# Another order for the seven products of a fast matrix product: the early pairs run M6, M7, M5, then M4 of the pair before, then M3

## The chip, the core and the metric

The kernel runs on one core of a Trainium2 chip. The metric is the device time of one launch in microseconds (us). The time before is 2344.93 us, the median of three runs (2343.69 to 2345.63).

## The reference

It is one layer of an encoder for two groups of tokens, 512 (`prompt`) and 1024 (`sample`), with shared weights and a width of 1024. A mixer with a convolution branch and a long-convolution branch comes first, then an MLP of width 4096. All is float32. The part that matters here is the first matrix of the MLP:

```
h = _ln(x) * (1.0 + scale2) + shift2
f = jnp.square(jax.nn.relu(jnp.einsum('bld,df->blf', h, mlp_w1[l]) + mlp_b1[l]))
f = jnp.einsum('blf,fd->bld', f, mlp_w2[l]) + mlp_b2[l]
x = _ln(DEEPNORM_ALPHA * x + gate2 * f, ln2_g[l], ln2_b[l])
```

## The kernel before

The kernel goes through both groups' mixers, then the MLP of the small group, and last the MLP of the large one. This last part is `up_seven` (the matrix `mlp_w1`, "up") and `down_seven` (`mlp_w2`). Both replace eight block products by seven, as Strassen's scheme does: tokens, contraction and output columns are each halved, and the seven products M1 to M7 work on sums and differences of the quarters (the table `SEVEN` names the weight piece and the token piece of each).

`up_seven` treats the 4096 output columns in 16 pairs n of two blocks of 128. One product is 12 matmuls of 128x512: four chunks of the contraction, and three matmuls for each, since a float32 operand is held as a high and a low part (`mm3`, and `split`, which makes the high part on ScalarE and the low part on VectorE). The token pieces are ready once (`h2_second`, tiles `pg`); the weight pieces of a pair are made by `up_weights` one to two pairs ahead, from four loads of 256 KB (tiles `raw` for even pairs, `xr` for odd ones): A11, A12, S1 and S2 in tiles `wt`, S3, S4 and A22 in tiles `pg`.

For the 14 early pairs (`NE`) the first loop does M1 and M2 already; M1 is written to the DRAM buffer `d_xs`, and the finished first block to `d_p`. The second loop fetches M1 back as `x` (line 1342, tile `sg`) and the block as `p11` (line 1357). It uses two accumulators in PSUM: `a` (tag `mm`) takes M6, then M5, then M3 on top of each other, and VectorE reads it after each of them (`keep()` gives `y` = x + M6 and `z` = x + M6 + M5, both tiles `xt`, and `p21` = x + all three, a tile `so`). `c` (tag `fx`) takes M7, is read for `p22`, then takes M4 on top and is read by `finish` for the block of slot 1. ScalarE applies the squared ReLU in two steps to every block, and the blocks and three sums of them (`s1`, `s2` and the `s4` of `finish`, tiles `sg`) are written to `d_p` by the queue of SyncE (`put`, line 1269). All DMAs of this part are issued by that one queue, in its order.

The order in the code is not the order on the engines. A scheduler puts every engine's instructions in a fixed row when the program is built, by priority (the place in the code; `soon` raises it) and by what its own model holds ready; buffers are given out at the same time. A product may so run earlier or later than it is written.

Of the kernel before, what the change touches and what calls it, by code (L numbers as in the profile page):

```python
# [173 lines left out]
class Enc:  # L174
# [1086 lines left out]
    def up_seven(self, g):  # L1261

        nc, v = self.nc, self.V
        put = lambda n, slot, t: nc.sync.dma_start(g.d_p[n, :, slot], t)
        NP = 16  # L1270
        ws = {n: {} for n in range(NP)}

        def c11(n, x, b):
            t = self.so()
            v.tensor_tensor(t, x, b, op=ALU.add)
            self.relu2(2 * n, t, t)
            put(n, 0, t)
            return t

        sums = self.h2_second(g, g.ss)  # L1280
        for n in range(NE):
            with self.soon(HW):
                for i in range(2):
                    ws[n]["A1" + "12"[i]] = self.piece(self.up_quarter(n, 0, i))
            for k in (1, 2):
                ps = self.mm_ps()
                self.up_product(g, ws[n], k, ps, True)
                if k == 1:
                    x = self.sg()
                    nc.scalar.activation(x, ps, AF.Copy)  # L1290
                    nc.sync.dma_start(g.d_xs[n], x)
                else:
                    c11(n, x, ps)
                if n >= NE - 6:
                    if n == NE - 6 and k == 1:
                        self.flush()
                    next(sums, None)
                yield 2.6
        self.flush()
        preps = {n: self.up_weights(n, ws[n], n >= NE) for n in range(NP)}  # L1300
        next(preps[0])
        next(preps[1])
        for _ in range(7):
            next(preps[0])
            next(sums, None)
        for _ in sums:
            pass
        last = None
        for n in range(NP):
            w = ws[n]  # L1310
            step = lambda: next(preps[n + 1], None) if n + 1 < NP else None
            early = n < NE
            a = self.mm_ps()

            def keep():
                t = self.xt()
                if early:
                    v.tensor_tensor(t, x, a, op=ALU.add)
                else:
                    nc.scalar.activation(t, a, AF.Copy)  # L1320
                return t

            def finish(last):
                y, c, s2, w0 = last
                self.up_product(g, w0, 4, c, False)
                t = self.so()
                v.tensor_tensor(t, y, c, op=ALU.add)
                f = 2 * n - 1
                self.relu2(f, t, t)
                put(n - 1, 1, t)  # L1330
                if s2 is not None:
                    s4 = self.sg()
                    v.tensor_tensor(s4, t, s2, op=ALU.subtract)
                    put(n - 1, 6, s4)

            if n + 2 < NP:
                with self.soon(20):
                    next(preps[n + 2])
            if early:
                x = self.sg()  # L1340
                with self.soon(40):
                    nc.sync.dma_start(x, g.d_xs[n])
            else:
                self.up_product(g, w, 1, a, True)
                x = keep()
            step()
            if last:
                finish(last)
                yield 2.6
            step()  # L1350
            self.up_product(g, w, 6, a, early)
            y = keep()
            step()
            if early:
                p11 = self.so()
                with self.soon(40):
                    nc.sync.dma_start(p11, g.d_p[n, :, 0])
                yield 0.0
            else:
                b = self.mm_ps()  # L1360
                self.up_product(g, w, 2, b, True)
                p11 = c11(n, x, b)
                yield 2.6
            step()
            self.up_product(g, w, 5, a, False)
            z = keep()
            yield 2.6
            step()
            c = self.fx_ps()
            self.up_product(g, w, 7, c, True)  # L1370
            p22 = self.so()
            v.tensor_tensor(p22, z, c, op=ALU.add)
            self.relu2(2 * n + 1, p22, p22)
            put(n, 5, p22)
            yield 2.6
            step()
            self.up_product(g, w, 3, a, False)
            p21 = self.so()
            if early:
                v.tensor_tensor(p21, x, a, op=ALU.add)  # L1380
                self.relu2(2 * n, p21, p21)
            else:
                self.relu2(2 * n, a, p21)
            s2 = None
            if n < N7:
                s1, s2 = self.sg(), self.sg()
                v.tensor_tensor(s1, p21, p22, op=ALU.add)
                put(n, 4, s1)
                v.tensor_tensor(p21, p11, p21, op=ALU.subtract)
                v.tensor_tensor(s2, s1, p11, op=ALU.subtract)  # L1390
                put(n, 2, s2)
            put(n, 3, p21)
            yield 2.6
            step()
            last = (y, c, s2, w)
        n = NP
        finish(last)
        yield 2.6
# [213 lines left out]
    def step(self, lane):  # L1612

        t = self.V.us
        try:
            next(self.side[lane][0])
        except StopIteration:
            self.side[lane].pop(0)
        self.spent[lane] += (self.V.us - t) / LANES[lane]
# [208 lines left out]
```

## Time and profile before

| what | value |
|---|---|
| median of three runs | 2344.93 us |
| the profiled execution | 2339.18 us, its span 2337.2 us |
| TensorE busy | 2238.0 us, 96% of the span |
| VectorE busy | 1904.4 us, 81% |
| ScalarE busy | 921.6 us, 39% |
| the second loop of `up_seven`, from pair 0 to pair 13 | 1773.39 to 1975.55 us of the span |

PE is TensorE, DVE is VectorE, ACT is ScalarE, SP is SyncE, whose queue issues the DMAs. In the rows further down the time of an instruction's start comes first, then its duration, and in brackets how long its engine had nothing to do before it and what ended that. Matmuls of one tile are merged into one row (x12). All of DVE's and PE's instructions have line 157, so they are told apart by their tiles: `xt<-sg,mm` is y or z, `so<-sg,mm` is p21, `so<-xt,fx` is p22 or the block of `finish`, `sg<-so` is s1.

### The profile page before, as it was taken

To read this page: it belongs to the slowest core of one execution; us is meant where nothing else is said; L and a number is where in the kernel's file an instruction comes from. 1 tells how busy PE (TensorE), PEld (TensorE's weight loads), DVE (VectorE), ACT (ScalarE), POOL (GpSimd) and SP (SyncE) were. 2 spreads that over 40 slices of the span, in tenths; PEclk is the share of its full clock that TensorE was granted. 3 is DMA by queue.
4 is the path that set the end of the run, shared out by engine and by line. 5 is a ranking of instruction groups with operands and counts; after the bars stand their busy time and mean duration, and the time that the engine had idled before them with its cause. 6 is when DMAs were issued, how large, how long until landed. Compare 5 with 4: busy or idle time off the path is not lost.

```text
span 2337.2 us, 32839 instructions
## 1 busy us (share of the span) xinstructions
PE 2238.0 (96%) x11492; PEld 1850.7 (79%) x11492; DVE 1904.4 (81%) x3694; ACT 921.6 (39%) x1521; POOL 54.0 (2%) x149
## 2 busy tenths in 40 slices
PE   6999999999999989979999999999999999999998
PEld 3878777787878877868888888789887777788886
DVE  5989798877989988888988877965988777577888
ACT  3464522422222223456443335222575345444430
POOL 2210100000000000000000000000000000000000
PEclk9999999999999999989999999999999999999999
DMA  6556425574446666534443326643675666876631
GB/s 246 180 159 189 138 79 188 196 240 155 153 149 211 217 213 219 191 129 139 138 128 107 121 77 234 207 149 117 223 238 185 207 214 212 287 247 206 216 117 69
DMA packets 201066, 414.34 MB, mean 177 GB/s; under 512 B 23321, under 2 KB 33739, under 8 KB 200389
## 3 DMA queue, kind: packets, MB, share of 16 engines
q1 hardware_dynamic: 200069, 411.24, 53.3%
q8 instruction: 90, 1.47, 0.3%
q0 software_dynamic: 832, 1.02, 0.2%
q14 instruction: 75, 0.61, 0.1%
HBM read 317.73 MB, written 94.43 MB: 176 GB/s over the span
## 4 chain that ended last, share of the span: by engine, by line
PE 74%; DVE 13%; DMA 7%; ACT 3%; issue 2%; SPq 1%; DVEq 0%; ACTq 0%
PE mm L157 55%; PE fx L157 16%; DVE fp L157 3%; PE tr L157 3%; DVE sg L157 2%; DVE pg L157 2%; DVE wt L157 2%; DMA sg<-d_xs 1%; DMA fp<-in_w_ada_dram 1%; DMA sg<-ks 1%; DVE st L157 1%; DVE cv L157 1%; DVE xt L157 1%; DVE sm L157 1%; DMA sg<-d_t 1%
## 5 line engine op out<-in xcount | busy, mean ns | idle before, releaser
L157 PE MATMUL mm<-pg,wt 128*128 128x512 f32 (+1 forms) x4776 | 1144.9, 392 | 13.2 <-ACT pg L214 5.1
L157 PEld LDWEIGHTS mm<-pg,wt 128*128 128x128 f32 x4776 | 878.9, 189 | 208.0 <-issue 17.3
L157 PE MATMUL mm<-wt,pg 128*128 128x512 f32 (+1 forms) x2556 | 486.3, 346 | 12.3 <-DVE pg L157 7.8
L157 PEld LDWEIGHTS mm<-wt,pg 128*128 128x128 f32 x2556 | 405.6, 191 | 71.4 <-DVE pg L157 9.7
L214 ACT ACTIVATE wt<-raw 128x512 fp32r<-128x512 f32 x430 | 268.4, 630 | 450.7 <-PE mm L157 357.8
L157 DVE TENSOR_TENSOR wt<-raw,wt 128x512 fp32r<-128x512 f32 x430 | 289.0, 683 | 55.5 <-ACT wt L214 53.9
L157 DVE SCALAR_TENSOR_TENSOR cv<-cv,pp 128x1024 f32<-128x1024 f32 (+1 forms) x288 | 289.1, 1009 | 10.9 <-ACT cv L851 7.0
L157 PEld LDWEIGHTS fx<-fp,fft 128*128 128x128 f32 x1536 | 180.4, 193 | 17.2 <-issue 8.9
L157 PE MATMUL fx<-fp,fft 128*128 128x128 f32 x1536 | 186.0, 278 | 2.0 <-DMA fft<-in_fft_sig_dram 0.8
L157 DVE TENSOR_TENSOR fp<-fp 128x256 f32<-128x256 f32 (+2 forms) x352 | 154.9, 476 | 24.9 <-ACT fp L380 14.6
L157 DVE TENSOR_TENSOR sg<-fx,sg 128x512 f32<-128x512 f32 (+1 forms) x162 | 98.4, 629 | 41.7 <-PE fx L157 26.7
L157 DVE TENSOR_TENSOR pg<-so,pg 128x512 fp32r<-128x512 f32 (+1 forms) x162 | 99.5, 624 | 38.7 <-ACT pg L214 32.8
L157 PE MATMUL fx<-pg,pg 128*128 128x512 f32 x492 | 119.6, 391 | 6.8 <-ACT pg L214 4.3
L157 PEld LDWEIGHTS fx<-pg,pg 128*128 128x128 f32 x492 | 92.6, 189 | 26.7 <-ACT pg L214 4.7
L214 ACT ACTIVATE pg<-so 128x512 fp32r<-128x512 f32 (+1 forms) x127 | 72.3, 576 | 90.9 <-DVE so L157 57.3
L157 PE MATMUL fx<-wt,pg 128*128 128x512 f32 x387 | 95.6, 389 | 0.3 <-DVE so L157 0.3
L1258 ACT ACTIVATE so<-so,pp 128x512 f32<-128x512 f32 x62 | 44.4, 719 | 130.3 <-DVE so L157 130.2
L157 DVE TENSOR_TENSOR sg<-sg 128x256 f32<-128x256 f32 (+2 forms) x187 | 82.0, 460 | 7.8 <-ACT sg L888 6.7
L157 PEld LDWEIGHTS fx<-wt,pg 128*128 128x128 f32 x387 | 72.6, 188 | 15.7 <-DVE so L157 0.7
L157 PE MATMUL mm<-pg,pg 128*128 128x512 f32 x300 | 73.9, 395 | 5.5 <-DVE xt L157 5.5
L380 ACT ACTIVATE fp<-fx 128x512 f32<-128x512 f32 x48 | 28.7, 598 | 123.7 <-PE fx L157 123.6
L157 DVE TENSOR_TENSOR pg<-pg,pg 128x1024 fp32r<-128x1024 f32 (+1 forms) x45 | 55.0, 1222 | 22.0 <-ACT pg L214 17.7
(175 smaller groups left out, 2163.1 us busy)
## 6 DMA issues: line engine op xcount, KB each, us to landing
raw<-in_mlp_w_dram SPq DMA_DIRECT2D x232, 256.0 KB
raw<-in_w_in_dram SPq DMA_DIRECT2D x144, 256.0 KB
xr<-in_mlp_w_dram SPq DMA_DIRECT2D x104, 256.0 KB
fp<-in_w_ada_dram SPq DMA_DIRECT2D x48, 512.0 KB
pg<-d_p SPq DMA_DIRECT2D x44, 512.0 KB
raw<-in_w_out_dram SPq DMA_DIRECT2D x64, 256.0 KB
d_p<-so SPq DMA_DIRECT2D x64, 256.0 KB
d_g<-so SPq DMA_DIRECT2D x48, 256.0 KB
```

Of the source, the lines that this page charges most:

```text
L157: return f(*args, **kw)
L214: self.nc.scalar.activation(hi, src, AF.Copy)
L380: nc.scalar.activation(outs[-1][:, 4 * (pr % 2):4 * (pr % 2) + 4].rearrange("p (j w) c -> p j w c", j=2), ps, AF.Copy)
L1258: nc.scalar.activation(out, src, AF.Relu, bias=self.pp[:, C_B1 + f:C_B1 + f + 1], scale=1.0)
```

## The change

For early pairs the code now writes M7 directly behind M6 instead of behind M5, and it calls `finish` of the pair before (M4, its sum, its ReLU and its two writes) behind the second block of the pair, in front of M3, instead of at the head of the pair. What is done stays the same.

```
-            if last:
+            if last and not early:
                 finish(last)
                 yield 2.6
             step()
...
                 with self.soon(40):
                     nc.sync.dma_start(p11, g.d_p[n, :, 0])
-                yield 0.0
+                c = self.fx_ps()
+                self.up_product(g, w, 7, c, True)
             else:
                 b = self.mm_ps()
                 self.up_product(g, w, 2, b, True)
                 p11 = c11(n, x, b)
-                yield 2.6
+            yield 2.6
             step()
             self.up_product(g, w, 5, a, False)
             z = keep()
             yield 2.6
             step()
-            c = self.fx_ps()
-            self.up_product(g, w, 7, c, True)
+            if not early:
+                c = self.fx_ps()
+                self.up_product(g, w, 7, c, True)
             p22 = self.so()
             v.tensor_tensor(p22, z, c, op=ALU.add)
             self.relu2(2 * n + 1, p22, p22)
             put(n, 5, p22)
+            if last and early:
+                finish(last)
             yield 2.6
```

TensorE, from pair 4 or so to pair 13, before: the last four rows of each name a token tile. 16893 ends M6 and the four `fx` rows are M7, both of pair n + 1; the four rows with 16606 to 16922 are M5, then M3 and M4, of pair n.

```order
L157 MATMUL mm<-pg_16893,wt 128x512 x3
L157 MATMUL fx<-pg_16610,pg_17657 128x512 x3
L157 MATMUL fx<-pg_16718,pg_17657 128x512 x3
L157 MATMUL fx<-pg_16818,pg_17657 128x512 x3
L157 MATMUL fx<-pg_16926,pg_17657 128x512 x3
L157 MATMUL mm<-pg_16606,wt 128x512 x3
L157 MATMUL mm<-pg_16714,wt 128x512 x3
L157 MATMUL mm<-pg_16814,wt 128x512 x3
L157 MATMUL mm<-pg_16922,wt 128x512 x3
L157 MATMUL mm<-pg,pg_17555 128x512 x12
L157 MATMUL fx<-pg,pg_17582 128x512 x12
```

The same place after the change:

```order
L157 MATMUL mm<-pg_16893,wt 128x512 x3
L157 MATMUL fx<-pg_16610,pg_17650 128x512 x3
L157 MATMUL fx<-pg_16718,pg_17650 128x512 x3
L157 MATMUL fx<-pg_16818,pg_17650 128x512 x3
L157 MATMUL fx<-pg_16926,pg_17650 128x512 x3
L157 MATMUL mm<-pg_16606,wt 128x512 x3
L157 MATMUL mm<-pg_16714,wt 128x512 x3
L157 MATMUL mm<-pg_16814,wt 128x512 x3
L157 MATMUL mm<-pg_16922,wt 128x512 x3
L157 MATMUL mm<-pg,pg_17555 128x512 x12
L157 MATMUL fx<-pg,pg_17582 128x512 x12
```

Nothing moved here but the number of a tile. Rows of TensorE moved only in the first four pairs, where M7 and M4 change places with parts of M6 and M5.

VectorE in one pair, before, from y and z (the first row) to s1 (the last). `raw` and `wt` rows make the weight pieces, and the row with 17657 is the low part of S3.

```order
L157 TENSOR_TENSOR xt<-sg,mm 128x512 x2
L157 TENSOR_TENSOR xt<-raw 128x512
L157 TENSOR_TENSOR so<-xt,fx 128x512
L157 TENSOR_TENSOR raw<-raw 128x512
L157 TENSOR_TENSOR raw<-xt,raw 128x512
L157 TENSOR_TENSOR pg_17657<-raw,pg_17657 128x512
L157 TENSOR_TENSOR so<-sg,mm 128x512
L157 TENSOR_TENSOR wt<-raw,wt 128x512
L157 TENSOR_TENSOR raw<-raw 128x512
L157 TENSOR_TENSOR wt<-xt,wt 128x512
L157 TENSOR_TENSOR sg<-so 128x512
```

The same place after the change:

```order
L157 TENSOR_TENSOR xt<-sg,mm 128x512 x2
L157 TENSOR_TENSOR xt<-raw 128x512
L157 TENSOR_TENSOR so<-xt,fx 128x512 x2
L157 TENSOR_TENSOR raw<-raw 128x512
L157 TENSOR_TENSOR raw<-xt,raw 128x512
L157 TENSOR_TENSOR so<-sg,mm 128x512
L157 TENSOR_TENSOR sg<-so,sg 128x512
L157 TENSOR_TENSOR wt<-raw,wt 128x512
L157 TENSOR_TENSOR raw<-raw 128x512
L157 TENSOR_TENSOR wt<-xt,wt 128x512
L157 TENSOR_TENSOR sg<-so 128x512
L157 TENSOR_TENSOR pg_17650<-raw,pg_17650 128x512
```

The sum of `finish` (the second `so<-xt,fx`) and its s4 (`sg<-so,sg`) now stand ahead of s1, where both stood behind it, and the low part of S3 went from ahead of s1 to directly behind it. Behind z, s1 was the tenth instruction and is the eleventh.

The queue of SyncE in one pair, before: the block p22, two weight loads, p11, s1, and then the load of x for the next pair, with what follows it.

```order
L1269 DMA d_p_95<-so 128x512
L1216 DMA raw<-in_mlp_w_dram 128x512 x2
L1357 DMA so<-d_p_95 128x512
L1269 DMA d_p_95<-sg 128x512
L1342 DMA sg<-d_xs_96 128x512
L1269 DMA d_p_95<-sg 128x512
L1269 DMA d_p_95<-so 128x512 x2
L1269 DMA d_p_95<-sg 128x512
L1216 DMA raw<-in_mlp_w_dram 128x512 x2
```

The same place after the change, from the load of p11 on (it comes at the end of the pair before now):

```order
L1357 DMA so<-d_p_95 128x512
L1269 DMA d_p_95<-so 128x512 x2
L1269 DMA d_p_95<-sg 128x512
L1216 DMA raw<-in_mlp_w_dram 128x512
L1269 DMA d_p_95<-sg 128x512
L1216 DMA raw<-in_mlp_w_dram 128x512
L1342 DMA sg<-d_xs_96 128x512
L1269 DMA d_p_95<-sg 128x512
L1269 DMA d_p_95<-so 128x512
L1216 DMA raw<-in_mlp_w_dram 128x512 x2
```

The two writes of `finish` and p11 went ahead, and one weight load now stands between the write of s1 and the load of x. That weight load refills the tile that the low part of S3 is made from, and so waits for that VectorE instruction.

## Rows read from the trace of the kernel before

**Rows 1.** Busy time in the fourteen early pairs: stretch, length, engines, clock, DMA share
```profile
1773.39:1975.55 202.16, 191.57 (x819) 151.76 (x818) 147.23 (x237) 86.35 (x147) 0.00 (x0) 1.00 0.61 203
```
**Rows 2.** Timeline of TensorE, one pair: M3, M4, M6, M7, M5
```profile
1866.96 3.01 PE L157 MATMUL mm<-pg,pg 128*128 128x512 f32 x12 [0.78 <-DVE xt L157]
1869.81 2.88 PE L157 MATMUL fx<-pg,pg 128*128 128x512 f32 x12
1872.53 2.88 PE L157 MATMUL mm<-pg,wt 128*128 128x512 f32 x12
1875.25 2.88 PE L157 MATMUL fx<-pg,pg 128*128 128x512 f32 x12
1879.26 3.04 PE L157 MATMUL mm<-pg,wt 128*128 128x512 f32 x12 [1.13 <-DVE xt L157]
```
**Rows 3.** Timeline of VectorE, the same pair: z, p21, s1, the next y
```profile
1866.21 0.69 DVE L157 TENSOR_TENSOR xt<-sg,mm 128x512 f32<-128x512 f32 x1 [3.10 <-PE mm L157]
...
1870.07 0.68 DVE L157 TENSOR_TENSOR so<-sg,mm 128x512 f32<-128x512 f32 x1
...
1872.48 0.68 DVE L157 TENSOR_TENSOR sg<-so 128x512 f32<-128x512 f32 x1
...
1878.52 0.69 DVE L157 TENSOR_TENSOR xt<-sg,mm 128x512 f32<-128x512 f32 x1 [1.75 <-DMA sg<-d_xs]
```
**Rows 4.** Timeline of SyncE's queue, the same pair: s1, then x
```profile
1873.19 0.33 SPq L1269 DMA_DIRECT2D d_p<-sg  x1
1873.56 0.42 SPq L1342 DMA_DIRECT2D sg<-d_xs  x1
```
**Rows 5.** Waits of VectorE, y on x's load: total, times, longest
```profile
DVE xt L157 <- DMA sg<-d_xs: 12.9, 12, 2.1
```
**Rows 6.** Chain that ended last: three loads of x, start and length
```profile
1781.59 3.95 DMA sg<-d_xs
...
1873.56 4.93 DMA sg<-d_xs
...
1904.82 5.09 DMA sg<-d_xs
```
**Rows 7.** Timeline of VectorE: z of pair 0 and of pair 12
```profile
1773.39 0.69 DVE L157 TENSOR_TENSOR xt<-sg,mm 128x512 f32<-128x512 f32 x1 [2.03 <-PE mm L157]
...
1959.71 0.69 DVE L157 TENSOR_TENSOR xt<-sg,mm 128x512 f32<-128x512 f32 x1 [3.25 <-PE mm L157]
```
**Rows 8.** Timeline of ScalarE, the pair of rows 2: the squares of p21
```profile
1871.64 0.63 ACT L1259 ACTIVATE so<-so 128x512 f32<-128x512 f32 x1
```
**Rows 9.** Timeline of SyncE's queue, pair 11: s1, a weight load, x
```profile
1951.74 0.33 SPq L1269 DMA_DIRECT2D d_p<-sg  x1
1952.34 0.33 SPq L1216 DMA_DIRECT2D xr<-in_mlp_w_dram  x1
1952.73 0.45 SPq L1342 DMA_DIRECT2D sg<-d_xs  x1
```
**Rows 10.** Timeline of VectorE, pair 11: z and the next y
```profile
1943.90 0.69 DVE L157 TENSOR_TENSOR xt<-sg,mm 128x512 f32<-128x512 f32 x1 [3.15 <-PE mm L157]
...
1955.78 0.69 DVE L157 TENSOR_TENSOR xt<-sg,mm 128x512 f32<-128x512 f32 x1 [0.46 <-DMA sg<-d_xs]
```
**Rows 11.** Table of a stretch just behind an issue of x
```profile
1874.46:1875.21 0.75, 0.75 (x5) 0.63 (x4) 0.75 (x2) 0.69 (x2) 0.00 (x0) 1.00 0.97 363
```
**Rows 12.** Timeline of TensorE: starts behind its two longest gaps in this part
```profile
1762.44 1.22 PE L157 MATMUL fx<-pg,pg 128*128 128x512 f32 x2 [4.26 <-ACT pg L214]
...
2010.45 3.02 PE L157 MATMUL fx<-pg,pg 128*128 128x512 f32 x12 [2.50 <-DVE so L157]
```
**Rows 13.** Table of the stretches around the first gap and behind the early pairs
```profile
1758.00:1763.00 5.00, 0.74 (x2) 0.50 (x2) 5.00 (x10) 2.20 (x5) 0.00 (x0) 0.75 0.71 238
...
1975.55:2010.00 34.45, 32.41 (x142) 26.13 (x140) 19.34 (x28) 20.12 (x34) 0.00 (x0) 1.00 0.87 284
2010.00:2337.00 327.00, 316.41 (x1392) 261.08 (x1392) 253.13 (x400) 120.07 (x173) 0.00 (x0) 0.99 0.55 183
```

More of the change, by code (lines that the diff above doesn't have):

```diff
@@ L1346, in up_seven @@
             step()
-            if last:
+            if last and not early:
                 finish(last)
@@ L1357, in up_seven @@
                     nc.sync.dma_start(p11, g.d_p[n, :, 0])
-                yield 0.0
+                c = self.fx_ps()
+                self.up_product(g, w, 7, c, True)
             else:
@@ L1362, in up_seven @@
                 p11 = c11(n, x, b)
-                yield 2.6
+            yield 2.6
             step()
@@ L1368, in up_seven @@
             step()
-            c = self.fx_ps()
-            self.up_product(g, w, 7, c, True)
+            if not early:
+                c = self.fx_ps()
+                self.up_product(g, w, 7, c, True)
             p22 = self.so()
@@ L1374, in up_seven @@
             put(n, 5, p22)
+            if last and early:
+                finish(last)
             yield 2.6
```

## The prediction

> **What bounds the kernel now.** The table of stretches comes first. From z of pair 0 to z of pair 13 TensorE works 191.57 of 202.16 us at a granted clock of 1.00 [rows 1]. So 10.6 us of gaps is all that a new order can win there while the matmuls stay.
>
> The timeline of TensorE shows where they are [rows 2]. In the scheduled row M7 already stands between M6 and M5 before the change, and so does the row of the next pairs. Two gaps are left in a pair: 0.78 us ahead of M3, which waits for VectorE to read z out of the accumulator that M3 adds to, and 1.13 us ahead of M5, which waits for y. M3, M4, M6 and M7 follow without a gap, about 2.72 us apart.
>
> VectorE's timeline tells why y is late [rows 3]: it starts 1.75 us after VectorE was free, released by the load of x. The waits add up to 12.9 us in 12 of 13 cases [rows 5], so M5's gap is x's landing, not the product M6 that y also reads (over by 1875.4 [rows 2]). The queue of SyncE shows what x stands behind [rows 4]: s1's write at 1873.19, then x at 1873.56. That write waits for s1 on VectorE, which ends at 1872.48 + 0.68 = 1873.16 [rows 3].
>
> So one ring sets a pair's length: z, the VectorE row up to s1, s1's write, x's issue, x's landing, y, M5, the next z. The chain of waits runs through these loads [rows 6], the first at 1781.59. Pair 0 to pair 12 takes (1959.71 − 1773.39)/12 = 15.53 us a pair [rows 7]. From y to z it is 3.8 us (M5's 3.04, with 0.74 to its start and a little behind it [rows 2, 3]), which leaves 11.70 from z to y. The twelve loads, from the first [rows 6] to the last [rows 9], are issued 7.68 us after z on average. The earliest is 7.35 (1873.56 − 1866.21 [rows 3, 4]); the first is 8.20 (1781.59 − 1773.39 [rows 6, 7]); the last 8.83 [rows 9, 10]. The rest, 4.02 us on average, passes from issue to y; it is 5.1 at most (4.96 and 5.12 for the two long loads [rows 6]) and 3.05 at least (1955.78 − 1952.73 [rows 9, 10]).
>
> **The change part by part.**
>
> M7 ahead of M5: nothing. The row on TensorE in a steady pair is the same before and after. The 13 gaps of 0.78 us ahead of M3 (10 us) are therefore not won: M3 and M4 still come as M5, M3, M4 and the accumulator is still read between M5 and M3. In the first four pairs M7 and M4 change places with parts of M6 and M5; each product is as long as any other, so this adds or removes one such gap at most, ±0.8 us, taken as 0.
>
> VectorE: the sum of `finish` and s4 now stand ahead of s1, S3's low part went behind it, net one more instruction. Between p21 and s1 the row goes on in steps of (1872.48 − 1870.07)/4 = 0.60 us [rows 3]. s1 before starts 6.27 after z in the pair shown, so 6.87 now, and ends at 7.55.
>
> ScalarE: one more instruction of the ReLU goes ahead of p21's square, which ends at 1872.27 [rows 8], 6.06 after z. With one instruction of some 0.55 us more it ends at 6.6, before 6.87, so s1 does not wait for it. If that margin of 0.27 is gone it is 0.3 us a pair at most, inside the bounds below.
>
> SyncE: s1's write goes at 7.57. Behind it the changed queue has a weight load ahead of x, and this load refills the tile that the low part of S3 reads. That instruction now comes directly behind s1: start 7.47, end 8.15. So the weight load is issued at 8.17, and x 0.39 us behind it, as in pair 11, where a weight load already stood there (1952.73 − 1952.34 [rows 9]): 8.56. Against the mean of 7.68 x goes out 0.88 us later. The other writes that moved ahead of s1 (p22, `finish`, s4) wait for work that is done earlier and don't hold x up. Queued behind the waiting weight load are x and the writes for which nobody on TensorE waits. S3's low part itself is ready at 8.15 after z; M7 which reads it starts at 1875.25 − 1866.21 = 9.04 [rows 2, 3]: 0.9 us of margin.
>
> The landing decides the sign, and the trace shows no pair of exactly this kind. The nearest rows bound it. From below: pair 11, the one with a weight load between s1's write and x, has 3.05 us to y, and the sum is 8.56 + 3.05 = 11.61, 0.09 less than now, −1.1 us in 12 pairs. From above: if the landing keeps its mean of 4.02, each pair is 0.88 longer, +10.6 us; with the longest, 5.12, it is 1.98, +23.8 us. Which is nearer? Lateness alone does little: the eight loads issued at 7.35 to 7.51 take 4.22 on average, the three at 8.0 to 8.2 take 4.04 (the first [rows 6], with 0.09 to y), 4.23 and 3.13. Pair 11 is nearer for its neighbours: in the pair of rows 4 there is nothing between the write and x, in pair 11 there is the weight load, as in the change. One row is thin, so I weigh it two to one against the mean: (2 × 3.05 + 4.02)/3 = 3.37. Then y comes at 11.93, +0.23 a pair, 12 × 0.23 = +2.8 us.
>
> Behind x the DMA engines are nearly full: 0.97 busy at 363 GB/s just after an issue [rows 11]. So the landing is a time in a crowd and no fixed latency.
>
> The Trainium skill has a rule for this, in "DMA: Bandwidth & Descriptors", section "Queues, rings and completion order": the mark by which a DMA reports its end is strongly ordered, so on each DMA engine it lands only when every earlier write of that engine has landed. By it x, issued 0.37 us behind a write to DRAM [rows 4], inherits that write's end, and inherits less now that the write is 0.99 us ahead with a load between. By it the sum would be that of pair 11, −1.1 us; the trace agrees in that one pair [rows 9, 10], and the rule alone does not say how much of the 4.02 us it explains.
>
> The time lost or won here goes to the end in full. Behind the early pairs TensorE is busy 32.41 of 34.45 and 316.41 of 327.00 us [rows 13], so nothing there takes up a delay. The clock: behind a gap of 4.26 us the first two matmuls took 1.22 us, and the stretch was granted 0.75, the level below full speed [rows 12, 13]; behind 2.50 us twelve matmuls took 3.02, as in any pair, and the clock stayed at 0.99 [rows 12, 13]. M5's gap grows from 1.13 to some 1.4 us by this estimate and to 3.1 at the worst bound, so I cost the clock at 0.
>
> The sum against the profiled execution: 2339.18 + 2.8 = 2342.0. That execution is 5.75 us below the median of the runs; on the median it is 2344.93 + 2.8 = **2347.7 us**.
>
> **The rivals.**
>
> A, slower: the landing does not shorten. x goes out 0.88 us later in each of 12 pairs and y follows: +10.6 us, 2355.5. For it: the two loads issued at 8.2 were 0.85 us later than most and landed no faster, and the same bytes are moved in a pair, so the crowd may be as thick. Against it: pair 11, and that the write stands farther ahead of x. It decides as soon as the landing exceeds 3.53 (8.56 + 3.53 is 0.39 over now, 4.7 us).
>
> B, faster: the crowd around x gets thinner. The two writes of `finish` and that of p22 now go out before s1, and p11's load after, so fewer bytes are in flight when x is. If x then needs under 2.7 us, y comes at 11.25 or before, −0.45 a pair, −5.4 us: 2339.5. The floor is TensorE: M7 ends at 1875.25 + 2.72 = 1877.97, 11.76 after z, M5 starts 0.74 behind y, so y before 11.02 wins nothing: −0.68 × 12 = −8.2, 2336.8. For it: the best landing seen is 3.05 with the weight load between. Against it: no landing in twelve was below that.
>
> C, the change does what its words say: M5, M4, M3 in turn, the 0.78 us ahead of M3 goes, −10 us, 2335. Against it: the scheduled row. Or the load of p11 now waits at the end of a pair for a write to land and blocks the queue: up to +10 us. Either is a way in which a step of mine would be wrong altogether.
>
> **How the numbers follow.** A measurement of this kernel can't tell less than about 0.2% (4.7 us) from no change. The forecast case, landing between 2.8 and 3.55 us, 0.44, nearly all of it within 0.2%: 2342 to 2350. A 0.35, all slower. B 0.16, faster, C 0.05, half and half. That gives faster 0.16 + 0.02 with little of the forecast case, 0.19; slower 0.35 + 0.03 and the upper edge of the forecast case, 0.40; the same 0.41. The range goes from 2338, which leaves out half of B, to 2357, which takes in A at the mean landing and leaves out its long landings: some 0.18 outside.
>
> **What would show it right or wrong.** In the changed kernel's profile: M3 still waits 0.78 us; x is issued some 8.5 us after z, directly behind a weight load, which is behind s1's write; from issue to y 3.4 us; z to z 15.75 us; y's waits for x still in nearly all pairs. The forecast is wrong if x leaves before 8.0 or after 9.2 after z, if y stops waiting for x, if M6 or M7 waits for a weight piece (`pg` or `wt`), or if TensorE's clock falls below 0.99 in a stretch of these pairs.

## The result and the profile after

The changed kernel takes 2354.94 us (median of six runs, 2348.28 to 2363.89), the kernel before 2344.31 in the same comparison (six runs): 10.6 us more, a ratio of 1.0054 with a 95% interval of 1.0037 to 1.0070. It is slower, by half a percent. The forecast was 2347.7 us; the range, 2338 to 2357, holds the time, but what came is the size of rival A and not of the likeliest case.

The profiled execution of the changed kernel took 2355.90 us, 16.7 more than that of before. That is more than the medians differ by: the execution of before lies 5.1 us under its median, the one of the changed kernel 1.0 over. The longest landing and two of the three slow starts of TensorE shown below did not come in a second profiled execution of the same instructions (`finish` alone, next section).

The table of stretches from z of pair 0 to z of pair 13, columns as in [rows 1], and one short stretch for later:

```profile
1773.94:1989.13 215.19, 196.27 (x820) 154.38 (x819) 145.92 (x236) 80.90 (x145) 0.00 (x0) 0.98 0.58 190
1886.00:1892.00 6.00, 5.42 (x12) 3.77 (x12) 0.54 (x1) 0.00 (x0) 0.00 (x0) 0.54 0.26 85
```

The fourteen pairs are 13.0 us longer (215.19 against 202.16 [rows 1]) for the same work, and the granted clock is no longer 1.00 throughout.

TensorE in one ordinary pair of the changed kernel, M3, M4, M6, M7, M5 as in [rows 2]:

```profile
1855.61 3.02 PE L157 MATMUL mm<-pg,pg 128*128 128x512 f32 x12 [0.78 <-DVE xt L157]
1858.47 2.88 PE L157 MATMUL fx<-pg,pg 128*128 128x512 f32 x12
1861.19 2.88 PE L157 MATMUL mm<-pg,wt 128*128 128x512 f32 x12
1863.91 2.88 PE L157 MATMUL fx<-pg,pg 128*128 128x512 f32 x12
1867.20 3.01 PE L157 MATMUL mm<-pg,wt 128*128 128x512 f32 x12 [0.41 <-DVE xt L157]
```

The row is that of before, with the wait of 0.78 us ahead of M3 still in it: what the change says it does has not happened on this engine. From pair 5 to pair 12 TensorE's row is the same in both kernels.

VectorE in the same pair: z, p21, s1, the low part of S3, the next y. These answer to [rows 3]:

```profile
1854.87 0.69 DVE L157 TENSOR_TENSOR xt<-sg,mm 128x512 f32<-128x512 f32 x1 [3.10 <-PE mm L157]
...
1858.67 0.69 DVE L157 TENSOR_TENSOR so<-sg,mm 128x512 f32<-128x512 f32 x1
...
1861.68 0.69 DVE L157 TENSOR_TENSOR sg<-so 128x512 f32<-128x512 f32 x1
1862.28 0.69 DVE L157 TENSOR_TENSOR pg<-xr,pg 128x512 fp32r<-128x512 f32 x1
...
1866.46 0.69 DVE L157 TENSOR_TENSOR xt<-sg,mm 128x512 f32<-128x512 f32 x1 [1.07 <-DMA sg<-d_xs]
```

And the queue of SyncE, s1's write, the weight load, x, as in [rows 4]:

```profile
1862.40 0.32 SPq L1269 DMA_DIRECT2D d_p<-sg  x1
1863.00 0.33 SPq L1216 DMA_DIRECT2D xr<-in_mlp_w_dram  x1
1863.38 0.44 SPq L1342 DMA_DIRECT2D sg<-d_xs  x1
```

s1 starts 6.81 us after z (6.27 in [rows 3]). Its write goes 7.53 after z (6.98 before), and x goes 0.98 behind the write (0.37 before), because the weight load between waits for S3's low part, which ends at 1862.97. x leaves 8.51 us after z.

VectorE's waits for x in pairs 0 to 12, columns as in [rows 5], then three landings of x from the chain that ended last, as in [rows 6]:

```profile
DVE xt L157 <- DMA sg<-d_xs: 23.1, 12, 4.4
```

```profile
1863.38 3.05 DMA sg<-d_xs
...
1878.76 6.41 DMA sg<-d_xs
...
1915.76 4.52 DMA sg<-d_xs
```

y waits 23.1 us for x instead of 12.9. Most landings are short now (3.05 here), but some are long. Behind three long waits TensorE starts slowly; its timeline, M5 of two pairs and one product behind the early pairs:

```profile
1885.93 5.49 PE L157 MATMUL mm<-pg,wt 128*128 128x512 f32 x12 [3.77 <-DVE xt L157]
...
1921.04 4.51 PE L157 MATMUL mm<-pg,wt 128*128 128x512 f32 x12 [1.88 <-DVE xt L157]
...
2024.76 4.54 PE L157 MATMUL fx<-pg,pg 128*128 128x512 f32 x12 [3.44 <-DVE so L157]
```

Twelve matmuls take 5.49 and 4.51 us instead of 3.0, and the granted clock from 1886 to 1892 is 0.54 (second line of the first fence), near the lower of its two levels (1.2 and 2.4 GHz).

Where the time went is seen best when each of the twelve pairs is cut in three: from z to x's issue, from there to y, and from y to the next z. The twelve pairs together take 198.90 us in the profile after and 186.32 in that of before, 12.6 us more: the issue is later by 0.81 a pair (+9.8), the landing shorter by 0.09 (−1.1), and from y to z it is 0.34 longer (+4.0, all of it in the two slow M5). Some 3 us more were lost behind these pairs, for the most part at 2024.76.

### The profile page after: what moved, and what is told of

It reads as the page before. It is cut to its first block, busy times and chain, and to the rows that moved or that the text cites. A ratio compares the mean times of both kernels' runs of the same rounds, so it can differ in the third digit from the quotient of the medians.

```text
span 2353.5 us, 32810 instructions
## 1 busy us (share of the span) xinstructions
PE 2241.9 (95%) x11492; PEld 1854.0 (79%) x11492; DVE 1903.5 (81%) x3694; ACT 917.2 (39%) x1521; POOL 54.2 (2%) x149
## 4 chain that ended last, share of the span: by engine, by line
PE 65%; DVE 17%; DMA 10%; issue 3%; ACT 2%; SPq 1%; DVEq 0%; ACTq 0%
PE mm L157 49%; PE fx L157 13%; DVE fp L157 4%; DVE sg L157 3%; DVE wt L157 3%; PE tr L157 2%; DVE pg L157 2%; DMA sg<-d_xs 2%; DMA pg<-d_p 1%; DVE cv L157 1%; DMA sg<-ks 1%; DMA fp<-in_w_ada_dram 1%; DVE so L157 1%; DMA fp<-in_dec_s_dram 1%; DVE st L157 1%
## 5 line engine op out<-in xcount | busy, mean ns | idle before, releaser
L157 DVE TENSOR_TENSOR xt<-sg,mm 128x512 f32<-128x512 f32 x28 | 19.2, 688 | 70.9 <-PE mm L157 47.4
```

The lines of the kernel that those rows point to most:

```text
L157: return f(*args, **kw)
```

## The experiments

The theory: a pair's length is z to x's issue to y to M5, and the change costs what it costs only because it sends x later. Its rival: the moved work itself, M7 or `finish`, costs the time on TensorE or VectorE.

**Each half of the change alone.** M7 alone:

```
+                c = self.fx_ps()
+                self.up_product(g, w, 7, c, True)
                 yield 0.0
...
-            c = self.fx_ps()
-            self.up_product(g, w, 7, c, True)
+            if not early:
+                c = self.fx_ps()
+                self.up_product(g, w, 7, c, True)
```

> The kernel before with only M7 written ahead of M5; finish stays where it was. Theory (the change costs what it costs because x leaves later: finish's sum and s4 stand ahead of s1, and a weight load stands between s1's write and x): the queue of SyncE and VectorE keep the rows of before, x leaves 7.7 us after z, and the time is that of before, 2344 us, within 3. Rival (M7's earlier place itself is what costs, by an earlier use of S3): over 2349.

Measured: 2341.41 us, against 2342.34 for the kernel before beside it; ratio 0.9993 (0.9980 to 1.0005). VectorE's waits for x in its trace, columns as above:

```profile
DVE xt L157 <- DMA sg<-d_xs: 10.9, 12, 1.5
```

Its time had to be that of before: on TensorE, VectorE, ScalarE and the queue of SyncE this kernel has the same instructions in the same order as the kernel before. The scheduler gave M7 its old place, so an earlier M7 as such is not tried here, and the run is a second measurement of the kernel before.

`finish` alone:

```
-            if last:
+            if last and not early:
                 finish(last)
...
             put(n, 5, p22)
+            if last and early:
+                finish(last)
```

> The kernel before with only finish moved behind the second block of the pair. Theory: this alone makes the changed rows on VectorE and SyncE, x leaves 8.5 us after z, landing 3.4 to 3.9 us on average, the time is that of the changed kernel, 2352 to 2358. Rival (both edits are needed, or M7 does it): 2344 to 2348.

Measured: 2353.94 us, ratio 1.0043 (1.0027 to 1.0060). SyncE's queue in one pair of it, s1's write, a weight load, x:

```profile
1834.75 0.32 SPq L1269 DMA_DIRECT2D d_p<-sg  x1
1835.35 0.33 SPq L1216 DMA_DIRECT2D xr<-in_mlp_w_dram  x1
1835.73 0.45 SPq L1342 DMA_DIRECT2D sg<-d_xs  x1
```

The 0.98 us from the write to x is here too, and on the same engines and the queue this kernel has the instructions of the changed kernel, in the same order. So the whole price belongs to the move of `finish`. The move of M7, for which a reader of the diff would look first, changes no engine's row.

**Only x's place on the queue.** In the kernel before, x is fetched a few lines later, so that it stands behind the writes of p21 and s2:

```
-            if early:
-                x = self.sg()
-                with self.soon(40):
-                    nc.sync.dma_start(x, g.d_xs[n])
-            else:
+            if not early:
...
             step()
+            if early:
+                x = self.sg()
+                with self.soon(40):
+                    nc.sync.dma_start(x, g.d_xs[n])
             self.up_product(g, w, 6, a, early)
```

> The kernel before with one thing moved in the early pairs: the load of x stands behind the writes of p21 and s2 on the queue of SyncE; the rows of TensorE, VectorE and ScalarE are those of before there. Theory (x's place on the queue sets the pair): x leaves some 9.2 us after z, 1.5 later than before, lands in 3.4 to 3.9 us, so a pair is 0.9 to 1.4 us longer, 11 to 17 us in twelve, and longer waits of TensorE may add up to 4 us by a lower clock: 2353 to 2363. Rival (the rows of VectorE, which the change moved and this kernel doesn't, cost the time): no more than 2346.

Measured: 2361.15 us (2352.62 to 2367.77), against 2342.89; ratio 1.0081 (1.0057 to 1.0105). SyncE's queue in its pair 1, the writes of s1, p21 and s2 and then x, and VectorE's waits:

```profile
1794.89 0.33 SPq L1269 DMA_DIRECT2D d_p<-sg  x1
1796.10 0.32 SPq L1269 DMA_DIRECT2D d_p<-so  x1
1796.70 0.32 SPq L1269 DMA_DIRECT2D d_p<-sg  x1
1797.07 0.44 SPq L1350 DMA_DIRECT2D sg<-d_xs  x1
```

```profile
DVE xt L157 <- DMA sg<-d_xs: 29.4, 12, 3.3
```

VectorE's and ScalarE's rows are those of before in all twelve pairs, TensorE's in pairs 6 to 10 (in the pairs ahead of these it has three more waits of 0.78 us in front of M3). From z of pair 6 to z of pair 11, where only the place of this DMA differs, the five pairs take 85.72 us instead of 77.69, 1.6 us more each (one slow start of M5, 1.4 us in all, is in it); the change adds 1.05 us to a pair on average. So the place of one DMA is enough to cost what the whole change costs; the two times, 1.0057 to 1.0105 and 1.0037 to 1.0070 of before, are not told apart. Whether the moved rows cost something besides is what the next runs ask.

**x earlier, the change kept.** In the changed kernel, x of the next pair is fetched directly behind the code of s1's write; the scheduler then puts it directly ahead of that write. Pair 0 fetches its own x as before; that part of the edit is left out here and in the last edit below:

```
...
                 put(n, 4, s1)
+                if n + 1 < NE:
+                    xn = self.sg()
+                    with self.soon(40):
+                        nc.sync.dma_start(xn, g.d_xs[n + 1])
```

> The changed kernel with x directly ahead of s1's write on the queue, in the same pair as before (not a pair early). Theory: x no longer waits for s1 on VectorE and not for the weight load, leaves some 6.4 us after z, 2.1 earlier than in the changed kernel; with a landing of 3.9 us y comes 10.3 us after z, no later than TensorE is ready for M5, so the waits for x all but vanish and it is level with x a whole pair early: 2327 to 2333. Rival (the landing stretches to the same end because the DMA engines are full until then): 2345 or more.

Measured: 2327.91 us, ratio 0.9939 (0.9926 to 0.9952), with x leaving even earlier than expected, 5.5 us after z. SyncE's queue in one pair (s4's write, x, s1's write) and the waits:

```profile
1833.82 0.32 SPq L1269 DMA_DIRECT2D d_p<-sg  x1
1834.18 0.46 SPq L1399 DMA_DIRECT2D sg<-d_xs  x1
1836.23 0.32 SPq L1269 DMA_DIRECT2D d_p<-sg  x1
```

```profile
DVE xt L157 <- DMA sg<-d_xs: 1.5, 1, 1.5
```

One wait of twelve is left: x, sent 3 us earlier than in the changed kernel, is there in time. On VectorE the sum of `finish` and s4 still stand ahead of s1, and they cost nothing that shows once x does not stand behind them. Not all of the gain is x's, though: the scheduler also gave this kernel another row on TensorE. Between M5 and M3 of a pair it put two matmuls into `fx` and two of the next M6, and M3 no longer waits:

```profile
1839.56 2.88 PE L157 MATMUL mm<-pg,wt 128*128 128x512 f32 x12
...
1843.22 3.01 PE L157 MATMUL mm<-pg,pg 128*128 128x512 f32 x12
```

How much of the gain is the load's and how much the row's was not tried apart.

The same twelve pairs of the profiles, ordered by when x leaves (means in us; the last column is the median of the runs, and the kernel before had medians of 2342.3 to 2344.3 beside them). The second and third line are two executions of the same instructions, and so are the fourth and fifth. The pairs of the first line are not quite the others': from z of pair 0 to z of pair 13 they hold 778 matmuls in place of 819.

| kernel | z to x's issue | issue to y | y to next z | 12 pairs | time |
|---|---|---|---|---|---|
| x ahead of s1 | 5.54 | 4.39 (not waited for) | 3.94 | 166.5 | 2327.9 |
| M7 alone | 7.62 | 3.91 | 3.80 | 184.0 | 2341.4 |
| before | 7.68 | 4.02 | 3.82 | 186.3 | 2344.3 |
| `finish` alone | 8.50 | 3.85 | 3.96 | 195.7 | 2353.9 |
| the change | 8.49 | 3.93 | 4.16 | 198.9 | 2354.9 |
| x behind s2 | 9.27 | 3.81 | 4.06 | 205.6 | 2361.2 |

From the second line to the last x leaves 1.65 us later and the time from issue to y is 0.10 us shorter: over nine tenths of the delay pass through.

**x a whole pair early, with and without the change.** In both kernels x of the next pair is fetched directly behind z in the code; in a steady pair it leaves 14.5 us (before) and 10.9 us (the change) ahead of y:

```
...
             z = keep()
+            if n + 1 < NE:
+                xn = self.sg()
+                with self.soon(40):
+                    nc.sync.dma_start(xn, g.d_xs[n + 1])
```

> The kernel before, with x fetched one pair ahead (issued behind z of the pair before, so some 11 us before its use). Theory: y no longer waits for x (12.9 us in 12 waits go), and only TensorE is left: 10.6 us of gaps in these pairs can go, so 2334 us, within 4. Rival (what y waits for is the row of VectorE up to s1, and x only seems last): no change, 2344.

> The changed kernel with x fetched one pair ahead. Theory: the change cost only through x, so with x early it is level with the kernel before with x early: 2334 us, within 4, some 21 below the changed kernel; no gap of y is long enough to lower the clock. Rival (finish ahead of s1 costs by itself, through VectorE): 10 us above the other kernel with x early, about 2344.

Measured: 2325.92 us for the kernel before with x early, ratio 0.9926 (0.9908 to 0.9944), and 2328.92 for the changed one, ratio 0.9945 (0.9926 to 0.9963). Both were expected at 2334; they are 5 to 8 us lower, and the next section says why. Since 3 us lay between them, both ran again:

> The kernel before with x a pair early, once more. Theory: 2326 us, within 3; y never waits for x; between M5 and M3 stands the rest of M7.

> The changed kernel with x a pair early, once more. Theory: on TensorE M4 of the pair before now stands between M5 and M3, without a gap in a pair (13.60 us for 60 matmuls against 13.77); that is 2 us in twelve pairs and less than the spread, so level with the other, 2324 to 2330. Rival (the change still costs outside these pairs): 3 us or more above the other.

Measured: 2328.40 (0.9932 to 0.9965 of before) and 2325.92 (0.9924 to 0.9948). The order of the two turned round, so they are not told apart, and the rival, that the moved work costs by itself, is out to within these few us. Both beat both kernels of this case, by 13 to 17 and by 26 to 29 us.

The scheduler gave these two kernels other rows on TensorE. The changed one with x early, in a stretch of one pair, M4, M3, M6, M7 and M5, then the table of one pair and of the twelve pairs:

```profile
1845.34 2.88 PE L157 MATMUL fx<-pg,pg 128*128 128x512 f32 x12
1848.06 2.88 PE L157 MATMUL mm<-pg,pg 128*128 128x512 f32 x12
1850.78 2.88 PE L157 MATMUL mm<-pg,wt 128*128 128x512 f32 x12
1853.50 2.88 PE L157 MATMUL fx<-pg,pg 128*128 128x512 f32 x12
1856.22 2.88 PE L157 MATMUL mm<-pg,wt 128*128 128x512 f32 x12
```

```profile
1845.54:1859.14 13.60, 13.60 (x61) 11.26 (x60) 11.17 (x18) 6.46 (x11) 0.00 (x0) 1.00 0.75 246
1780.10:1940.74 160.64, 160.64 (x709) 132.81 (x708) 133.38 (x215) 76.70 (x131) 0.00 (x0) 1.00 0.69 230
```

Here the words of the change have come true: M4 stands between M5 and M3, and no wait is left in the pair. In the kernel before with x early, M7 is cut in two and its rest stands there instead (M7's first seven matmuls, M5, M7's last five; M3 follows):

```profile
1854.30 1.75 PE L157 MATMUL fx<-pg,pg 128*128 128x512 f32 x7
1855.90 3.00 PE L157 MATMUL mm<-pg,wt 128*128 128x512 f32 x12
1858.74 1.30 PE L157 MATMUL fx<-pg,pg 128*128 128x512 f32 x5
```

```profile
1845.17:1858.94 13.77, 13.77 (x61) 11.13 (x60) 11.12 (x19) 6.62 (x11) 0.00 (x0) 1.00 0.65 230
```

So by the traces the change's order is worth 0.17 us a pair, 2 us in twelve, and only where x is early; the times don't show it. Why the scheduler puts M4 behind M3 while x is late was not looked into.

## Why the prediction was right in kind and wrong in size

**The ring** was right: y waits for x in all twelve pairs of the changed kernel, and the kernels of the table stand in the order in which they send x.

**M7 ahead of M5, taken as nothing**: right; alone it leaves every row in place (0.9993). A count beside it was wrong: not 13 gaps of 0.78 us stand ahead of M3 in the trace of before (10 us), but seven (5.5 us). TensorE's waits for y and z there, columns as in [rows 5], are these seven and five ahead of M5; by this count rival C's −10 us is −5.5:

```profile
PE mm L157 <- DVE xt L157: 10.4, 12, 1.5
```

**VectorE, ScalarE and SyncE**: right nearly to the digit. s1 was to start 6.87 after z and started 6.81; p21's square, which was to leave it 0.27 us, ended at 1861.36, 0.32 ahead of it; the weight load was to go at 8.17 and went at 8.13; x was to leave at 8.56 and left at 8.51 in the pair shown and 8.49 on average.

**The landing was mis-sized**, and it is the term that made the likeliest case wrong. I took 3.37 us, one odd pair (pair 11 [rows 9, 10]) weighed two to one against a mean of twelve. It was 3.93 (3.85 with `finish` alone, the same instructions), so +0.72 a pair and 8.6 in twelve in place of +0.23 and 2.8. Rival A, the landing that does not shorten, gave +10.6. That the medians differ by just these 10.6 us is luck in part: issue and landing make 8.6, and the rest is slow starts of TensorE and time behind the pairs, which A does not have. The bound from the mean was the better guide: pair 11's neighbours on the queue made it look like the case, but the landing of a single pair scatters by more than the effect that I read out of it. Of the twelve landings after, eight are between 3.08 and 3.55 and one is 4.57, together 3.48 on average; the three others, 4.54 to 6.43, met a packet of instructions, of which the last section tells.

The rule of the Trainium skill that I weighed ("DMA: Bandwidth & Descriptors", section "Queues, rings and completion order") points the right way: those nine landings are 0.34 shorter than the ten of before that met no such packet (3.82), and with x directly behind s2's write again they are 3.73. That is a third of a us, and x was sent 0.81 later for it. The thinner crowd of rival B would shorten them as well; the two were not tried apart.

**The clock, costed at nothing**, was wrong. I reasoned from one gap of 2.50 us that left it alone [rows 12], and I took a granted 0.75 for a level [rows 13]: it is the mean of 5 us in which the clock fell, and from 1760.50 to 1763.00 alone it is 0.50. In the profile after, M5 ran at the lower level behind gaps of 3.77 and 1.88 us and lost 2.5 and 1.5 us by it; with `finish` alone and with x behind s2 it was so in one and two pairs of twelve. So these three executions paid some 1.5 to 4 us for it in the twelve pairs, and that of before paid nothing; this may be part of why the changed kernel's six runs lie 15 us apart.

**That 10.6 us of gaps is all that an order can win** was wrong, though nothing in the forecast hung on it; two of my expectations did. A busy time counts a row of matmuls ahead of a gap in full, up to 3.0 us for what takes 2.72 in a row. In the pairs with x early 709 matmuls take 160.64 us, 0.2266 each; the 819 of [rows 1] so need 185.6 of 202.16 us, and 16.5 us were to be had. The kernels with x early got 13 to 17. The Trainium skill says this of the profiler ("Perfetto Trace Analysis", section "Identifying Performance Opportunities"): matmul busy share is no good measure of how near TensorE is to its limit, because matmuls are pipelined; this trace agrees that it is none, with 16.5 us to be had where the busy time shows 10.6. The Trainium skill's reason is that pipelined instructions look smaller in a trace; here the busy time is too large, 191.57 us for matmuls that need 185.6.

**The signs set down**: M3's wait of 0.78 us, x's issue at 8.5 and y's waits came. From issue to y it was 3.93 and not 3.4, z to z 16.58 and not 15.75, and the clock fell to 0.54 in a stretch of these pairs, one of the signs of being wrong.

**Open**: VectorE's later s1 (0.55 us of the delay in an ordinary pair) and the weight load ahead of x (0.61) were only read from the traces; they were not tried apart.

## What to carry to other kernels

Where one engine waits for a load, look at what stands ahead of that load on its queue before looking at the order on the engine that waits: here a load of data whose write had been issued 94 us or more before (from the load at 1781.6 on) stood behind a write that waited for the arithmetic of the pair. Fetching it earlier, with the row on TensorE that the scheduler then chose, won 13 to 17 us; the change of the products' order by itself won nothing. A late issue passed through to the end nearly one to one; do not count on a crowded transfer to make it up because one row did.

Read in the order of the instructions whether a change of the code moves the engine that it speaks of. This one left TensorE's row alone in most pairs and moved VectorE's and the queue's, and half of it, M7's move, left every row alone.

## What the runs showed of the hardware

A landing can hang on one of the sixteen DMA engines. The long landing at 1878.76 is the clearest. The DMA page from 1880.00 to 1882.25 has a packet of a queue of instructions in it (queue and kind, packets, MB, share of sixteen engines over these 2.25 us), and the table of stretches from x's issue on shows what followed (DMA share and GB/s are the last two columns):

```profile
q8 instruction: 1, 0.02, 7.7%
```

```profile
1878.76:1882.25 3.49, 3.40 (x16) 2.47 (x14) 1.99 (x4) 0.00 (x0) 0.00 (x0) 1.00 0.88 292
1882.25:1884.00 1.75, 0.00 (x0) 0.00 (x0) 0.00 (x0) 0.00 (x0) 0.00 (x0) 1.00 0.15 48
```

7.7% of sixteen engines over 2.25 us is 2.8 us of one engine for that single packet. Then the transfers were all but over (share 0.15, most of it where the next load starts): from 1882.25 to 1883.70 only four packets of 2 KB start, one after the other, and y still waited. In five profiles (before, the change, each half, x behind s2), 11 of 60 landings had a packet of this queue, 16 KB each, in flight with them: they took 4.91 us on average, the other 49 took 3.68. Fourteen of the 49 met an 8 KB packet of a second queue of instructions, q14, and took 3.68 as well. That the packet is the cause is read from the course of the one landing, since the trace does not say which load a packet belongs to; for the others it is a coincidence in time. A load that was just in time seems to pay for this; x a pair early met such packets as well, and y never waited.

The length of a gap alone doesn't say whether TensorE's clock falls. Over the ten traces, from the early pairs to some 60 us behind them, the twelve matmuls behind gaps of 1.88, 2.06, 2.08, 2.18, 2.36, 2.62 and 2.65 us took 4.45 to 4.62 us, and behind gaps of 1.91, 2.16 (twice), 2.27, 2.50 and 2.82 us they took 3.01 to 3.06; behind 3.44, 3.77 and 3.93 us they took 4.54 to 5.49.
